# Down projection of an encoder layer as a block product in seven multiplications

## Chip, cores and metric

The kernel runs on one core of one Trainium2 chip. The metric is the device time of one execution in microseconds (us), lower is better. TensorE is called PE, VectorE DVE, ScalarE ACT and GpSimd POOL, as in the profile; SP is the engine that issues most transfers.

## What is computed

One layer of a bidirectional encoder over 768 token rows (512 of a prompt, 256 of a sample), width 1024, all in float32. The change touches the last stage alone, the down projection of the ConvFFN with its residual and the final norm:

```python
uv = dwconv(jnp.matmul(h, w_up), ffn_conv_w, ffn_conv_b, ...)   # (768, 6144)
gate, val = jnp.split(uv, 2, axis=-1)
x = x + jnp.matmul(jax.nn.gelu(gate) * val, w_down)             # (768, 3072) @ (3072, 1024)
y = rmsnorm(x, final_g)
```

## The kernel before

**Numbers in two parts.** Each float32 operand of a large matmul is split into a rounded high part (ACT copies it to the matmul type) and the rest (a subtraction on DVE or POOL). A product is three matmuls: high by high, low by high, high by low. They add up in a PSUM bank.

**Up projection.** `window(j, pend)` (line 1162), 24 times, makes one tile of 128 gate and 128 value channels for all 768 tokens. It is already a block product in seven multiplications: the operands of the next window are sums of weight blocks, made on POOL by `UpSet.sums` (lines 899 to 902) and split by `UpSet.pair` (lines 924, 925). Each window has seven calls of `prod` (line 1096) of twelve 128x384 matmuls. Beside them ACT and DVE finish the tile of the window before (`pend`, class `Gate`): taps of the convolution, gelu, product. `spill` (line 1145) writes the finished tile `vl` to DRAM (`actd`).

**Down projection.** The last loop (line 1317) goes over two halves `h` of 384 tokens. For each half, 24 steps `k` over the 3072 channels: `act` loads the half tile of activations back (line 1274) and splits it (ACT line 1277, DVE line 1278), `unit("down", ...)` loads a 128x1024 slab of `w_down` and splits it (ACT line 106, DVE line 107), and 18 matmuls of 128x512 (three token tiles `c`, two column halves `hf`, three parts, `mms`, line 1330) add into six banks that stay open over the half. Every slab of `w_down` is thus loaded and split twice. After each half `add_res` (line 1300) adds the six banks to the residual rows `x2`, which were loaded back from DRAM.

**Final norm.** `final(c)` (line 1302) for one tile of 128 tokens: two squares with row sums on ACT (line 838), a POOL product with the gain (line 1306), a chain of tiny DVE and ACT instructions for the root (`tok_rstd`, lines 845 to 853), a DVE product (line 1309), an ACT product (line 1310) and two output transfers, issued on ACT's queue. Those of the first half's tiles stand in steps 1 to 3 of the second half; those of the second half come at the end, where the last `TAIL = 4` steps are done tile by tile.

**What sets the order.** In this part each engine runs its instructions in the order of the code. A buffer of a pool is handed on when its last reader is done, so an engine can run ahead of PE by as many steps as there are buffers: eight of tag `v` for the split activations (gate and value tiles, squares and `z` of `final` share them), 14 of tag `u` for split weights, three of `raw` for loaded weights. PSUM has five banks of tag `b` and three of tag `c`.

Of the kernel before, what the change touches and what calls it, by code (L numbers as in the profile page):

```python
# [8 lines left out]
F32 = mybir.dt.float32  # L9
F32R = mybir.dt.float32r  # L10
I32 = mybir.dt.int32
AF = mybir.ActivationFunctionType
# [21 lines left out]
def kernel(  # L34
# [43 lines left out]
    def r32(ap):  # L78
        return ap.bitcast(F32R)
# [10 lines left out]
    def plan(key, src, n):  # L90
        order.append((key, src, n))
# [3 lines left out]
    def issue_to(i):  # L95
        while issued[0] < min(i, len(order)):
            key, src, n = order[issued[0]]
            issued[0] += 1
            raw = rawtile("w_raw")
            nc.sync.dma_start(raw[:, 0:n], src)  # L100
            if key[0] == "gw":
                t = wtile("w_gw")
                hi, lo = t[:, 0:n], t[:, 528 : 528 + n]
            else:
                hi, lo = wtile("w_hi")[:, 0:n], wtile("w_lo")[:, 0:n]
            A.activation(r32(hi), raw[:, 0:n], AF.Copy)  # L106
            (V if key[0] == "down" else G).tensor_tensor(r32(lo), raw[:, 0:n], hi, op=SUB)  # L107
            units[key] = (r32(hi), r32(lo))
# [19 lines left out]
    for i in range(8):  # L128
        plan(("out", i), w_out[i], 1024)

    for h in range(2):
        for k in range(24):
            plan(("down", h, k), w_down[k], 1024)

# [963 lines left out]

    actd = dram.tile([24, P, NP], F32, name="actd")
    ffs = ExitStack()  # L1100
    ffp = None

    def etile(name):
        return ffp.tile([P, HT], F32, tag="e", name=name, bufs=6)

    def vtile(name):
        return ffp.tile([P, NP], F32, tag="v", name=name, bufs=8)

    def gtile(name):
        return ffp.tile([P, 1024], F32, tag="g", name=name, bufs=2)  # L1110

    fw, fb = cs["fw"], cs["fb"]

    class Gate:
# [29 lines left out]
        def spill(self):  # L1144
            nc.sync.dma_start(actd[self.j], self.vl[:])

        def rest(self):

            self.mid(1, 0)
            self.mid(0, 0)  # L1150
            self.taps(0, 0)
            self.gelu(0)
            self.mid(0, 1)
            self.taps(1, 0)
            self.mult(0)
            self.mid(1, 1)
            self.taps(0, 1)
            self.gelu(1)
            self.taps(1, 1)
            self.mult(1)  # L1160

    def window(j, pend):
# [3 lines left out]
        if j + 2 < 24:  # L1166
            sets[j + 2] = UpSet(j + 2)
        p1, q, wv = etile("p1"), etile("q"), etile("wv")
        gt, vl = vtile("gt"), vtile("vl")
# [7 lines left out]
        if nx:  # L1177
            nx.hi_g()
        else:
            act_to(1)  # L1180
        A.activation(p1[:], ba, AF.Copy)
# [7 lines left out]
        if nx:  # L1189
            nx.pair(0)  # L1190
        else:
            issue_down(1)
        pend.mid(1, 1)
# [17 lines left out]
        if nx:  # L1211
            nx.pair(1)
            nx.hi_22()
            nx.lo_22()()
        else:
            act_to(2)
            issue_down(2)
# [47 lines left out]

    acts = {}
    aorder = [(h, k) for h in range(2) for k in range(24)]
    atop = [0]

    def act_to(i):  # L1270
        while atop[0] < min(i, 48):
            h, k = aorder[atop[0]]
            t = ffp.tile([P, HT], F32, tag="ar", name="a_raw", bufs=3)
            nc.sync.dma_start(t[:], actd[k, :, h * HT : h * HT + HT])
            x = vtile("act")
            ah, al = x[:, 0:HT], x[:, HT:NP]
            A.activation(r32(ah), t[:], AF.Copy)
            V.tensor_tensor(r32(al), t[:], ah, op=SUB)
            acts[h, k] = (ah, al)
            atop[0] += 1  # L1280

    def act(h, k):
        act_to(aorder.index((h, k)) + 3)
        return acts.pop((h, k))

    down0 = [o[0] for o in order].index(("down", 0, 0))

    def issue_down(n):
        issue_to(down0 + n)

    for j in range(1, 24):
        pend = window(j, pend)


    fgb = gtile("fgb")

    def add_res(c, ps):
        for hf in range(2):
            xx = x2[c][hf]
            V.tensor_tensor(xx, ps[hf], xx, op=ADD)  # L1300

# [11 lines left out]

    def dbank(tag):
        return pm["p"].tile([P, 512], F32, tag=tag, name="d", bufs=5 if tag == "b" else 3)

    for h in range(2):
        xr = granule("xr")[:].rearrange("p a b -> p (a b)")
        for c in range(3):
            for hf in range(2):  # L1320
                x2[3 * h + c][hf] = xr[:, 1024 * c + 512 * hf : 1024 * c + 512 * hf + 512]
        bk = {}
        tags = "bbbbbc" if h == 0 else "ccbbbb"

        def mms(a, u, c, hf, k):
            if (c, hf) not in bk:
                bk[c, hf] = dbank(tags[2 * c + hf])
            (ah, al), (wh, wl) = a, u
            for i, (x, w) in enumerate(((ah, wh), (al, wh), (ah, wl))):
                PE.matmul(bk[c, hf], lhsT=r32(x[:, c * P : c * P + P]), rhs=w[:, hf * 512 : hf * 512 + 512],  # L1330
                          start=k == 0 and i == 0, stop=k == 23 and i == 2)

        late = []
        for k in range(24 - TAIL):
            a, u = act(h, k), unit("down", h, k)
            for c in range(3):
                for hf in range(2):
                    if h == 0 and k < 2 and (c, hf) == (2, 1):
                        late.append((a, u, c, hf, k))
                    else:  # L1340
                        mms(a, u, c, hf, k)
            if h == 0 and k == 0:
                pend.rest()
            if h == 0 and k == 2:
                pend.spill()
            if h == 0 and k == 4:
                nc.sync.dma_start(fgb[:], fin_g.to_broadcast([P, D]))
            if k == 1:
                for m in late:
                    mms(*m)  # L1350
            if h == 1 and 1 <= k < 4:
                final(k - 1)
            if 6 <= k < 18 and k % 2 == 0:
                c, hf = divmod((k - 6) // 2, 2)
                nc.sync.dma_start(x2[3 * h + c][hf], x2d[3 * h + c, :, hf * 512 : hf * 512 + 512])
        rest = [(act(h, k), unit("down", h, k), k) for k in range(24 - TAIL, 24)]
        for c in range(3):
            for hf in range(2):
                for a, u, k in rest:
                    mms(a, u, c, hf, k)  # L1360
            add_res(3 * h + c, [bk[c, 0], bk[c, 1]])
            if h:
                final(3 * h + c)
    ffs.close()
# [75 lines left out]
```

## Time and profile before

| | |
|---|---|
| median of three runs | 954.53 us (952.23 to 955.11) |
| the profiled execution | 954.8 us, its span 953.1 us |
| PE, DVE, ACT, POOL busy | 95%, 66%, 53%, 42% of the span |
| mean granted TensorE clock | 0.986 |
| up projection, windows 1 to 23 | to 743.5 us from the start of the span |
| down projection | 743.5 to 945.9 us |
| last output | to 953.1 us |

Times in the rows below are microseconds from the start of the span, durations of one instruction are in nanoseconds where the column says so. A row of an idle time names what ended it.

### The profile page before, as it was taken

The page shows a single profiled execution, that of the slowest core. Times are in us where ns is not written, and L with a number is a line of the kernel's source. Part 1 is how long each engine was busy: PE and PEld are TensorE (multiplying, and loading weights), DVE is VectorE, ACT ScalarE, POOL GpSimd, SP SyncE. Part 2 cuts the span into 40 slices and gives each one's busy share as a digit, 9 for nine tenths or more (in the row PEclk, how much of TensorE's full clock was granted, in tenths as well). Part 3 has the DMA queues.
Part 4 walks back from the last instruction along what each step waited for, and adds up shares of the span by engine and source line. Part 5 has one row for each costly group of instructions (what it writes and reads, how often), then busy time and mean ns, then how long its engine had stood idle before and what let it go on. Part 6 is the DMA issues. An engine that isn't in the chain of part 4 may idle for free.

```text
span 953.1 us, 13653 instructions
## 1 busy us (share of the span) xinstructions
PE 908.2 (95%) x5066; PEld 828.5 (87%) x5066; DVE 631.4 (66%) x1176; ACT 500.4 (53%) x827; POOL 403.9 (42%) x261
## 2 busy tenths in 40 slices
PE   8896999999899899899999999999999999999996
PEld 6796877898899677899999999999999788888885
DVE  6788999437778757576766766767667664346523
ACT  6464565055354055575665766756655454336513
POOL 4622333256433516687667667676672000010001
PEclk9998999999899999999999999999999999999999
DMA  6411111063235212323223133132221697428901
GB/s 221 144 46 64 45 67 45 13 157 89 78 87 190 89 47 87 125 70 122 95 88 122 69 114 118 66 122 84 100 78 48 221 355 248 147 91 275 315 29 67
DMA packets 42419, 110.47 MB, mean 116 GB/s; under 512 B 4976, under 2 KB 12656, under 8 KB 42352
## 3 DMA queue, kind: packets, MB, share of 16 engines
q1 hardware_dynamic: 40320, 106.38, 33.6%
q10 hardware_dynamic: 2032, 3.22, 1.0%
q8 instruction: 40, 0.66, 0.3%
q14 instruction: 27, 0.22, 0.1%
HBM read 93.78 MB, written 15.79 MB: 115 GB/s over the span
## 4 chain that ended last, share of the span: by engine, by line
PE 73%; DVE 16%; POOL 3%; ACT 3%; issue 2%; DMA 2%; SPq 0%; POOLq 0%; ACTq 0%; DVEq 0%
PE b L1096 34%; PE d L1330 20%; PE big L141 6%; PE sm L832 3%; PE sm L742 3%; PE b L1035 2%; DVE xc L350 2%; PE sm L451 1%; DVE w L375 1%; POOL hq L955 1%; POOL w_lo L107 1%; DVE thi L386 1%; DVE nt L197 1%; DVE xgl L252 1%; DVE rs L199 1%
## 5 line engine op out<-in xcount | busy, mean ns | idle before, releaser
L1096 PE MATMUL b<-hq,w_sh 128*128 128x384 f32 (+2 forms) x792 | 199.9, 334 | 3.6 <-POOL hq L955 2.7
L1330 PE MATMUL d<-w_hi,act 128*128 128x512 f32 x576 | 179.9, 393 | 2.2 <-DVE vl L1142 1.1
L925 POOL TENSOR_TENSOR w_sl<-w_S,w_sh 128x1024 fp32r<-128x1024 f32 x48 | 115.7, 2410 | 115.7 <-ACT w_sh L924 115.7
L1096 PEld LDWEIGHTS b<-hq,w_sh 128*128 128x128 f32 x792 | 143.1, 189 | 4.3 <-POOL hq L955 3.0
L1096 PE MATMUL b<-hq,w_sl 128*128 128x384 f32 (+2 forms) x396 | 132.3, 334 | 0.0
L1330 PEld LDWEIGHTS d<-w_hi,act 128*128 128x128 f32 x576 | 107.8, 188 | 28.0 <-DVE vl L1142 1.5
L106 ACT ACTIVATE w_hi<-w_raw 128x1024 fp32r<-128x1024 f32 (+1 forms) x77 | 81.0, 1056 | 90.7 <-PE d L1330 52.8
L107 POOL TENSOR_TENSOR w_lo<-w_raw,w_hi 128x1024 fp32r<-128x1024 f32 (+1 forms) x29 | 74.5, 2577 | 118.6 <-ACT w_hi L106 75.0
L1330 PE MATMUL d<-w_lo,act 128*128 128x512 f32 x288 | 112.7, 391 | 0.0
L1096 PE MATMUL b<-hq,w_gh 128*128 128x384 f32 x384 | 99.1, 339 | 0.0
L1306 POOL TENSOR_TENSOR z<-xr,fgb 128x512 f32<-128x512 f32 x6 | 7.8, 1294 | 213.0 <-ACT sq L838 126.5
L107 DVE TENSOR_TENSOR w_lo<-w_raw,w_hi 128x1024 fp32r<-128x1024 f32 x48 | 58.8, 1225 | 56.3 <-ACT w_hi L106 55.2
L1096 PEld LDWEIGHTS b<-hq,w_sl 128*128 128x128 f32 x396 | 74.8, 189 | 0.0
L1096 PEld LDWEIGHTS b<-hq,w_gh 128*128 128x128 f32 x384 | 70.2, 189 | 0.0
L1096 PE MATMUL b<-hq,w_gl 128*128 128x384 f32 x192 | 65.0, 339 | 0.0
L1330 PEld LDWEIGHTS d<-w_lo,act 128*128 128x128 f32 x288 | 54.1, 188 | 12.2
L1124 ACT ACTIVATE cv<-vl,col 128x512 f32<-128x512 f32 (+1 forms) x48 | 32.1, 669 | 49.1 <-DVE vl L1220 47.8
L141 PE MATMUL big<-xgh,w_hi 128*128 128x512 f32 x208 | 54.8, 344 | 2.4 <-DVE kT L762 2.3
L1096 PE MATMUL b<-hq,w_v 128*128 128x384 f32 x288 | 54.4, 337 | 0.9 <-DVE wv L1252 0.9
L141 PE MATMUL big<-xgl,w_hi 128*128 128x512 f32 x208 | 53.5, 338 | 0.0
L141 PE MATMUL big<-xgh,w_lo 128*128 128x512 f32 x208 | 53.3, 337 | 0.0
L1096 PEld LDWEIGHTS b<-hq,w_v 128*128 128x128 f32 x288 | 50.7, 188 | 1.0 <-ACT w_gh L906 1.0
(301 smaller groups left out, 2054.3 us busy)
## 6 DMA issues: line engine op xcount, KB each, us to landing
w_raw<-in_w_down_dram SPq DMA_DIRECT2D x48, 512.0 KB, 4.9
w_g<-in_w_up_dram SPq DMA_DIRECT2D x24, 512.0 KB, 4.1
w_v<-in_w_up_dram SPq DMA_DIRECT2D x24, 512.0 KB, 4.9
actd<-vl SPq DMA_DIRECT2D x24, 384.0 KB, 2.6
a_raw<-actd SPq DMA_DIRECT2D x48, 192.0 KB, 5.1
w_raw<-in_w_fm_dram SPq DMA_DIRECT2D x13, 512.0 KB, 3.4
w_raw<-in_w_out_dram SPq DMA_DIRECT2D x8, 512.0 KB, 5.3
M<-md SPq DMA_DIRECT2D x12, 256.0 KB, 4.1
```

What stands on the lines that cost most here:

```text
L106: A.activation(r32(hi), raw[:, 0:n], AF.Copy)
L107: (V if key[0] == "down" else G).tensor_tensor(r32(lo), raw[:, 0:n], hi, op=SUB)
L141: PE.matmul(dst, lhsT=w, rhs=x[:, lo:hi], start=first and i == 0, stop=last and i == 2,)
L197: V.tensor_tensor(t[:], y, y, op=MUL)
L350: V.scalar_tensor_tensor(xc[:, d0:d1], xs[:, d0 + o : d1 + o], cw[:, 4 * j + i : 4 * j + i + 1], xc[:, d0:d1], op0=MUL, op1=ADD)
L742: PE.matmul(ps[:, 0:256], lhsT=x[:, p0 : p0 + P], rhs=w[:, o : o + 256], start=n == 0, stop=n == 23)
L832: PE.matmul(ps[:, 0:512], lhsT=a, rhs=w[:, hf * 512 : hf * 512 + 512], start=first and k == 0 and i == 0, stop=last and k == n - 1 and i == 2)
L925: G.tensor_tensor(r32(sl[:, 0:1024]), x, sh[:, 0:1024], op=SUB)
L1035: PE.matmul(ps[:, 0:512], lhsT=a, rhs=w[:, hf * 512 : hf * 512 + 512], start=k == 0 and i == 0, stop=k == 3 and i == 2)
L1096: PE.matmul(t[:, a:b], lhsT=wt, rhs=r32(hq[:, k, off + a : off + b]), start=first and n == 0, stop=n == len(seq) - 1, skip_group_check=True)
L1124: A.activation(t[:, 0 : hi - lo], x[:, lo:hi], AF.Identity, bias=fb[:, m : m + 1], scale=fw[:, 48 + m : 49 + m])
L1330: PE.matmul(bk[c, hf], lhsT=r32(x[:, c * P : c * P + P]), rhs=w[:, hf * 512 : hf * 512 + 512], start=k == 0 and i == 0, stop=k == 23 and i ...
```

## The change

The product of activations A (768 x 3072) and weights B (3072 x 1024) is cut in two by two blocks: A by token half (first index, 384 tokens) and by even or odd channel tile (second index), B by even or odd channel tile and by column half. Seven products of size 384 x 1536 x 512 take the place of eight:

- S1 = A21 + A22, S3 = A11 - A21, S2 = S1 - A11, S4 = A12 - S2, and from the weights B12 - B11, B22 - B12, B22 - (B12 - B11) and (B22 - (B12 - B11)) - B21.
- In the order of `DORD`: 1 is A11 B11, 2 is A12 B21, 5 is S1 (B12 - B11), 7 is S3 (B22 - B12), 6 is S2 (B22 - B12 + B11), 3 is S4 B22, 4 is A22 times the last weight sum.

Each product has twelve steps (pairs of channel tiles); a step is 9 matmuls of 128x512 (three token tiles, three parts) into three banks. After a product, `into` adds each bank on DVE to all residual blocks that it belongs to: 4, 1, 2, 2, 3, 1 and 1 blocks for each of three banks, 42 additions in all.

The activation sums are made by `Gate.sums` on POOL, four subtractions or additions of 128x384 for each pair of windows, and written to DRAM; a step of the down projection then loads one 128x384 operand. The weight blocks are loaded once (48 of 128x512) and stay; sums of weights are made in place on POOL. The low part of a weight operand is a POOL subtraction in products 1, 2 and 4; in the others ACT copies the operand to a PSUM bank (`wc`) and DVE subtracts from there. All six residual tiles are loaded at the start of window 23 (`down_begin`). The work left of the last tile and the additions of banks 1 and 2 of a product stand, one entry a step, in the list `todo`; so do `final(0)` to `final(2)`, after product 3. Tag `v` has seven buffers in place of eight.

```diff
-            (V if key[0] == "down" else G).tensor_tensor(r32(lo), raw[:, 0:n], hi, op=SUB)
+            G.tensor_tensor(r32(lo), raw[:, 0:n], hi, op=SUB)
...
+        def sums(self):
+
+            if self.j % 2 == 0:
+                return
+            p = self.j // 2
+            u, v = evens.pop(p), self.vl
+            a11, a21, a12, a22 = u[:, 0:HT], u[:, HT:NP], v[:, 0:HT], v[:, HT:NP]
+            t = ffp.tile([P, 4 * HT], F32, tag="sp", name="sp", bufs=1)
+            s1, s3, s2, s4 = (t[:, HT * i : HT * i + HT] for i in range(4))
+            G.tensor_tensor(s1, a21, a22, op=ADD)
+            G.tensor_tensor(s3, a11, a21, op=SUB)
+            G.tensor_tensor(s2, s1, a11, op=SUB)
+            G.tensor_tensor(s4, a12, s2, op=SUB)
+            spq.append(lambda: nc.sync.dma_start(actd[p, :, 3 * HT : 7 * HT], t[:]))
...
         A.activation(gt[:, 0:HT], ba, AF.Copy)
+        pend.sums()
         prod(bd, w, 4, False)
         V.tensor_tensor(vl[:, 0:HT], bd, q[:], op=ADD)
+        if not nx:
+            prep_to(2)
...
+    DORD = (1, 2, 5, 7, 6, 3, 4)
+    steps = [(i, p) for i in DORD for p in range(12)]
+    ahead = 3
...
+    def down_begin():
+
+        st = wpool.tile([P, 2048], F32, tag="S", name="x_S", bufs=1)
+        homes = [gtile("x_g")[:], gtile("x_g")[:], st[:, 0:1024], st[:, 1024:2048],
+                 rawtile("x_raw")[:, 0:1024], rawtile("x_raw")[:, 0:1024]]
+        load_to(2)
+        for c in range(NT):
+            x2[c] = [homes[c][:, 512 * hf : 512 * hf + 512] for hf in range(2)]
+            nc.sync.dma_start(homes[c], x2d[c])
...
+    def load_to(n):
+
+        while done_load[0] < min(n, len(steps)):
+            i, p = steps[done_load[0]]
+            if i in NEW:
+                wblock(NEW[i], p)
+            t = etile("a_raw")
+            nc.sync.dma_start(t[:], actd[p, :, HT * AOFF[i] : HT * AOFF[i] + HT])
+            xd[i, p] = t
+            done_load[0] += 1
...
+    def prep_to(n):
+
+        while done_prep[0] < min(n, len(steps)):
+            i, p = steps[done_prep[0]]
+            load_to(done_prep[0] + 1)
...
+            elif i == 5:
+                G.tensor_tensor(b11, b12, b11, op=SUB)
+                w = b11
...
             x = vtile("act")
             ah, al = x[:, 0:HT], x[:, HT:NP]
+            wt = wtile("w_s")
+            wh, wl = wt[:, 0:512], wt[:, 528:1040]
+            A.activation(r32(wh), w, AF.Copy)
+            if i in (1, 2, 4):
+                G.tensor_tensor(r32(wl), w, wh, op=SUB)
+            else:
+                ct = cbank("wc")
+                A.activation(ct[:], w, AF.Copy)
+                V.tensor_tensor(r32(wl), ct[:], wh, op=SUB)
             A.activation(r32(ah), t[:], AF.Copy)
             V.tensor_tensor(r32(al), t[:], ah, op=SUB)
...
+    def into(i, c, b):
+        for th, hf in INTO[i]:
+            xx = x2[3 * th + c][hf]
+            if i == 4:
+                V.scalar_tensor_tensor(xx, b, -1.0, xx, op0=MUL, op1=ADD)
+            else:
+                V.tensor_tensor(xx, b, xx, op=ADD)
...
+    for n, i in enumerate(DORD):
+        bk = [bank(), bank(), None]
+        for p in range(12):
+            s = 12 * n + p
+            last = i == 4 and p >= 12 - TAIL
+            if not (last and p > 12 - TAIL):
+                prep_to(s + 1 + ahead)
+            if i == 4 and p == 12 - TAIL:
+                prep_to(len(steps))
+            if not last:
+                for c in range(2):
+                    dmms(bk[c], i, p, c)
+                if p:
+                    if p == 1:
+                        bk[2] = bank()
+                        dmms(bk[2], i, 0, 2)
+                    dmms(bk[2], i, p, 2)
+            if todo:
+                todo.pop(0)()
...
+        if i == 4:
             for c in range(3):
+                for p in range(12 - TAIL, 12):
+                    dmms(bk[c], i, p, c)
+                into(i, c, bk[c])
+                final(3 + c)
+        else:
+            into(i, 0, bk[0])
+            todo += [(lambda i=i, c=c, b=bk[c]: into(i, c, b)) for c in (1, 2)]
+            if i == 3:
+                todo += [(lambda c=c: final(c)) for c in range(3)]
```

How the change moves instructions shows at two places. The first is ACT, where the final norm of the first half's tiles stands among the preparations of later steps (`w_hi` or `w_s` is a weight split, `act` an activation split, `sq`, `rt` and `z` belong to `final`). Before, in the second half's steps 1 to 3:

```order
L106 ACTIVATE w_hi<-w_raw 128x1024
L838 ACTIVATE sq,s_8286<-xr 128x512 x2
L848 ACT_TABLE_LOAD
L848 ACTIVATE rt<-s_8286,pre 128x1
L1310 ACTIVATE z<-z,rt 128x512
L1311 DMA out_dram<-z 128x512
L1312 DMA out_dram<-xr 128x512
L1277 ACTIVATE act<-a_raw 128x384
L106 ACTIVATE w_hi<-w_raw 128x1024
L838 ACTIVATE sq,s_8335<-xr 128x512 x2
```

Now, in the third, fourth and fifth step of the last product:

```order
L1354 ACTIVATE act<-a_raw 128x384
L834 ACTIVATE sq,s_9134<-x_g 128x512 x2
L844 ACT_TABLE_LOAD
L844 ACTIVATE rt<-s_9134,pre 128x1
L1373 ACTIVATE z<-z,rt 128x512
L1374 DMA out_dram<-z 128x512
L1375 DMA out_dram<-x_g 128x512
L1347 ACTIVATE w_s<-w_d 128x512
L1354 ACTIVATE act<-a_raw 128x384
L834 ACTIVATE sq,s_9171<-x_g 128x512 x2
```

One preparation still stands between two finals, but it is now that of a step of 9 matmuls, where it was that of a step of 18. The second place is POOL from the last window into the down projection (`w_S` and `w_sl` are weights of the up projection, `sp` the activation sums). Before:

```order
L899 TENSOR_TENSOR w_S<-w_g,w_v 128x512
L900 TENSOR_TENSOR w_S<-w_v 128x512
L901 TENSOR_TENSOR w_S<-w_S,w_g 128x512
L902 TENSOR_TENSOR w_S<-w_g,w_S 128x512
L925 TENSOR_TENSOR w_sl<-w_S,w_sh 128x1024 x2
L1306 TENSOR_TENSOR z<-xr,fgb 128x512 x6
```

Now:

```order
L921 TENSOR_TENSOR w_sl<-w_S,w_sh 128x1024 x2
L1159 TENSOR_TENSOR sp<-vl 128x384
L1160 TENSOR_TENSOR sp<-vl 128x384
L1161 TENSOR_TENSOR sp<-sp,vl 128x384
L1162 TENSOR_TENSOR sp<-vl,sp 128x384
L1349 TENSOR_TENSOR w_s<-w_d,w_s 128x512 x8
...
L1349 TENSOR_TENSOR w_s<-w_d,w_s 128x512 x16
L1329 TENSOR_TENSOR w_d<-w_d 128x512 x12
L1332 TENSOR_TENSOR w_d<-w_d 128x512 x12
L1335 TENSOR_TENSOR w_d<-w_d 128x512 x12
L1338 TENSOR_TENSOR w_d<-w_d 128x512 x12
L1349 TENSOR_TENSOR w_s<-w_d,w_s 128x512 x6
```

POOL had only the six products of the final norm in this stage; it now has an instruction of 128x512 for every step, and the four sums of a pair follow the weights of every second window.

## Rows read from the trace of the kernel before

**Rows 1.** The page: busy time and share of each engine.
```profile
PE 908.2 (95%) x5066; PEld 828.5 (87%) x5066; DVE 631.4 (66%) x1176; ACT 500.4 (53%) x827; POOL 403.9 (42%) x261
```

**Rows 2.** The page: the chain that ended last, by engine.
```profile
PE 73%; DVE 16%; POOL 3%; ACT 3%; issue 2%; DMA 2%; SPq 0%; POOLq 0%; ACTq 0%; DVEq 0%
```

**Rows 3.** That chain in order of time: start, length, what, how many.
```profile
752.53 0.70 DVE vl L1142
...
753.27 192.65 PE d L1330 x834
945.94 0.70 DVE xr L1300
```

**Rows 4.** Stretches of the down projection: length, busy time by engine, clock, DMA share, GB/s.
```profile
743.50:753.30 9.80, 7.64 (x33) 5.33 (x31) 7.54 (x11) 5.83 (x9) 0.00 (x0) 1.00 0.59 214
753.30:945.90 192.60, 192.60 (x834) 156.46 (x834) 94.62 (x141) 81.29 (x124) 7.76 (x6) 1.00 0.58 196
763.00:783.00 20.00, 20.00 (x89) 16.28 (x88) 14.05 (x18) 12.20 (x16) 0.00 (x0) 1.00 0.98 351
```

**Rows 5.** The page's transfer issues: KB each, median us from issue to landing.
```profile
a_raw<-actd SPq DMA_DIRECT2D x48, 192.0 KB, 5.1
```

**Rows 6.** Groups of instructions in two windows, 700 to 724: busy us, mean ns, idle before.
```profile
L919 DVE TENSOR_TENSOR w_gl<-wc,w_gh 128x512 fp32r<-128x512 f32 x4 | 2.7, 679 | 0.0
L902 POOL TENSOR_TENSOR w_S<-w_g,w_S 128x512 f32<-128x512 f32 x2 | 2.6, 1297 | 0.2
L931 ACT ACTIVATE w_v<-w_v 128x512 fp32r<-128x512 f32 x2 | 1.2, 614 | 0.0
L935 ACT ACTIVATE wc<-w_v 128x512 f32<-128x512 f32 x2 | 1.2, 602 | 0.0
```

**Rows 7.** POOL in order of time in the windows: start, length, idle before.
```profile
704.72 2.40 POOL L925 TENSOR_TENSOR w_sl<-w_S,w_sh 128x1024 fp32r<-128x1024 f32 x1 [3.39 <-ACT w_sh L924]
...
719.46 2.40 POOL L925 TENSOR_TENSOR w_sl<-w_S,w_sh 128x1024 fp32r<-128x1024 f32 x1 [3.84 <-ACT w_sh L924]
722.59 2.41 POOL L925 TENSOR_TENSOR w_sl<-w_S,w_sh 128x1024 fp32r<-128x1024 f32 x1 [0.73 <-ACT w_sh L924]
```

**Rows 8.** Groups of instructions, 743.5 to 953.1: the same columns.
```profile
L1278 DVE TENSOR_TENSOR act<-a_raw,act 128x384 fp32r<-128x384 f32 x46 | 25.4, 553 | 6.3 <-ACT act L1277 6.3
L1277 ACT ACTIVATE act<-a_raw 128x384 fp32r<-128x384 f32 x46 | 23.7, 514 | 7.8 <-DMA a_raw<-actd 4.0 <-PE d L1330 1.3 <-issue 1.0
L1300 DVE TENSOR_TENSOR xr<-d,xr 128x512 f32<-128x512 f32 x12 | 8.3, 690 | 33.6 <-PE d L1330 33.6
L838 ACT ACTIVATE sq<-xr 128x512 f32<-128x512 f32 x12 | 7.5, 624 | 21.5 <-DVE xr L1300 19.4 <-DVE pre L845 2.1
```

**Rows 9.** POOL and DVE in order of time, an early stage and a window.
```profile
59.57 0.96 DVE L376 SCALAR_TENSOR_TENSOR thi<-thi,xc 128x768 f32<-128x768 f32 x1
63.10 2.55 POOL L107 TENSOR_TENSOR w_lo<-w_raw,w_hi 128x1056 fp32r<-128x1056 f32 x1 [16.64 <-PE sm L451]
63.35 3.12 DVE L375 SCALAR_TENSOR_TENSOR w<-w,thr 128x768 f32<-128x768 f32 x1
719.93 0.49 DVE L1133 SCALAR_TENSOR_TENSOR cv<-gt,col,cv 128x255 f32<-128x255 f32 x1
```

**Rows 10.** ACT in order of time, finals in the second half's first steps.
```profile
850.41 1.28 ACT L848 ACT_TABLE_LOAD   x1 [4.08 <-DVE pre L845]
...
856.22 0.61 ACT L838 ACTIVATE sq<-xr 128x512 f32<-128x512 f32 x1
...
860.06 0.53 ACTq L1312 DMA_DIRECT2D out_dram<-xr  x1
...
862.03 0.62 ACT L838 ACTIVATE sq<-xr 128x512 f32<-128x512 f32 x1
```

**Rows 11.** The last output transfer, issued on SP.
```profile
949.28 0.34 SPq L1312 DMA_DIRECT2D out_dram<-xr  x1
```

**Rows 12.** A PE wait before the windows and the clock behind it.
```profile
383.66 0.39 PE L1096 MATMUL b<-hq,w_sh 128*128 128x256 f32 x1 [2.66 <-POOL hq L955]
384.00:386.00 2.00, 2.00 (x12) 2.00 (x11) 1.84 (x7) 1.17 (x4) 2.00 (x2) 0.50 0.46 184
```

More of the change, by code (lines that the diff above doesn't have):

```diff
@@ L1097, in prod @@
                       start=first and n == 0, stop=n == len(seq) - 1, skip_group_check=True)
-    actd = dram.tile([24, P, NP], F32, name="actd")
+    actd = dram.tile([12, P, 7 * HT], F32, name="actd")
     ffs = ExitStack()
@@ L1106, in vtile @@
     def vtile(name):
-        return ffp.tile([P, NP], F32, tag="v", name=name, bufs=8)
+        return ffp.tile([P, NP], F32, tag="v", name=name, bufs=7)
     def gtile(name):
@@ L1264 @@
     pend = Gate(0, gt, vl)
[L1266 to L1274, printed above, removed]
+    DORD = (1, 2, 5, 7, 6, 3, 4)
+    AOFF = {1: 0, 2: 1, 4: 2, 5: 3, 7: 4, 6: 5, 3: 6}
+    steps = [(i, p) for i in DORD for p in range(12)]
+    ahead = 3
@@ new lines, in wblock @@
+    def wblock(b, p):
+        if (b, p) not in wB:
+            if b == 11:
+                if p % 2 == 0:
+                    wu[p // 2] = wtile("w_d")
+                t = wu[p // 2][:, 528 * (p % 2) : 528 * (p % 2) + 512]
+            else:
+                if p % 6 == 0:
+                    wu[b, p // 6] = granule("w_d")[:].rearrange("p a b -> p (a b)")
+                t = wu[b, p // 6][:, 512 * (p % 6) : 512 * (p % 6) + 512]
+            r, c = divmod(b, 10)
+            nc.sync.dma_start(t, w_down[2 * p + r - 1, :, 512 * c - 512 : 512 * c])
+            wB[b, p] = t
+        return wB[b, p]
@@ L1278, in act_to @@
             V.tensor_tensor(r32(al), t[:], ah, op=SUB)
[L1279 to L1289, printed above, removed]
+            ops[i, p] = (r32(ah), r32(al), r32(wh), r32(wl))
+            done_prep[0] += 1
+            load_to(done_prep[0] + 2)
     for j in range(1, 24):
         pend = window(j, pend)
-    fgb = gtile("fgb")
@@ L1297, in add_res @@
[L1297 to L1300, printed above, removed]
+    fgb = rawtile("fgb")
     def final(c):
@@ L1312, in final @@
         (nc.sync if c == NT - 1 else nc.scalar).dma_start(out[c, :, 512:1024], xx)
[L1314 to L1335, printed above, removed]
-            for c in range(3):
[L1337 to L1363, printed above, removed]
@@ new lines, with dmms @@
+    INTO = {1: ((0, 0), (0, 1), (1, 0), (1, 1)), 2: ((0, 0),), 5: ((0, 1), (1, 1)), 7: ((1, 0), (1, 1)),
+            6: ((0, 1), (1, 0), (1, 1)), 3: ((0, 1),), 4: ((1, 0),)}
+    def into(i, c, b):
[3 more added lines that the diff above has]
+                V.scalar_tensor_tensor(xx, b, -1.0, xx, op0=MUL, op1=ADD)
+            else:
+                V.tensor_tensor(xx, b, xx, op=ADD)
+    def dmms(b, i, p, c):
+        ah, al, wh, wl = ops[i, p]
+        for n, (x, w) in enumerate(((ah, wh), (al, wh), (ah, wl))):
+            PE.matmul(b[:], lhsT=x[:, c * P : c * P + P], rhs=w,
+                      start=p == 0 and n == 0, stop=p == 11 and n == 2)
```

62 lines of the change are left out of this document (38 added, 24 removed).

## The prediction

> **What bounds the kernel now.** I read the page first: PE is busy for 95% of the span [rows 1], and PE instructions make 73% of the chain that ended last [rows 2]. The chain in order of time says the same of the stage that changes: from 753.27 us it is one run of 834 down-projection matmuls without a gap, 192.65 us long [rows 3], so one 128x512 matmul starts each 192.65 / 834 = 0.231 us. [...] The first 30 of the 864 matmuls were no such run. They took 9.77 us, from 743.5 us to 753.27 us, where 30 x 0.231 = 6.93 us would do: the chain stood in the last tile's convolution and product (DVE L1142), which held a bank that the half wanted [rows 3, 4]. So PE's count of matmuls sets this stage as long as the operands are ready.
>
> **The change part by part.** The sum is made against the profiled execution, 954.8 us, which lies 0.3 us above the median of the three runs.
>
> *Fewer matmuls.* Seven products of 12 steps of 9 matmuls are 756 where there were 864, all 128x512: 108 x 0.231 = **24.9 us less**. Nothing hides behind PE here, so this counts in full.
>
> *The start.* The first product needs three banks instead of six, the third in its second step, so the wait for the last tile's work goes: 9.77 - 6.93 = **2.8 us less**. What is late next is POOL's queue. It holds eight low parts and then the last pair's four sums, which wait for DVE's last product of the tile, some four steps or 9 us in; four sums of 1.0 us and a low part later, at 14 to 15 us, step 8 is ready, which PE wants at 8 x 2.08 = 16.6 us. On SP's queue the spill of these sums holds the loads of step 11: issued at 14 us, landed 5.1 us later [rows 5], split in 2 us, against 11 x 2.08 = 22.9 us. Both have 1 to 2 us to spare. Bounds 0 and 2 us, taken **0.5 us more**.
>
> *The windows.* Sums of 128x384 have no row. POOL needs 1.30 us for 512 columns [rows 6] and 2.41 us for 1024 [rows 7], so about 1.0 us for 384, 4.1 us in every second window. A window is 719.46 - 704.72 = 14.74 us, and POOL sits idle 3.84 + 0.73 us in it, waiting for ACT [rows 7]. The sums push the next window's weight sums by 4.1 us, which takes that wait and some of ACT's slack; the split weights are used a window later. Taken at 0; without that cover, up to 1 us in each of 11 windows.
>
> *Preparing a step.* PE needs 9 x 0.231 = 2.08 us for a step. ACT spends 0.60 us on the high part, 0.60 us on the copy to PSUM (products 5, 7, 6, 3) and 0.51 us on the activation, 1.7 us [rows 6, 8]. DVE spends 0.55 us on the activation and, in those products, 0.68 us on the weight [rows 6, 8]. POOL has 1.30 us in every step. A step loads at most 459 kB, 221 GB/s at this pace, against 351 GB/s seen [rows 4]. Each is under 2.08 us, but two of them are not independent: a DVE instruction that reads two SBUF operands does not run beside POOL. One that takes 0.96 us alone took 3.12 us from 63.35 us: it waited for the POOL instruction that ended at 65.65 us. One that reads an operand from PSUM took its 0.49 us beside a POOL instruction of 2.40 us [rows 7, 9]. So the activation's split and POOL's instruction take turns, 0.55 + 1.30 = 1.85 us a step together: still under 2.08 us, but a lost lead comes back at only 0.2 us a step. [...]
>
> *The additions.* 42 x 0.69 us [rows 8] = 29 us of DVE in place of 8. They stand in DVE's queue: the first of a product waits for its bank, and later splits queue behind it. When it waits, DVE has prepared the three steps beyond the product, so that PE has some 7.6 us of work; after product 1 (four additions a bank) the third split comes 8.3 + 3 x 0.55 us plus waits for POOL later, when PE wants it after 11.8 us. Products 1 and 6 (three a bank, beside 1.23 us of splits a step) come near the margin, the others do not. Bounds 0 and 6 us, taken **1.5 us more**.
>
> *Finals of the first half's tiles.* Each holds ACT from its squares to its last transfer's issue, 860.06 + 0.53 - 856.22 = 4.4 us, and the first loads a table for 1.28 us more [rows 10]. Before, a step was 18 matmuls, 4.2 us, and finals 5.8 us apart (862.03 - 856.22) were caught up by the splits made ahead [rows 10]. Now a step is 2.08 us. Let t count from the first matmul of the last product. The first squares run at once, the root waits until DVE has added bank 2 and split step 77, about t = 2.5. From there table 1.3, the rest of the final 4.4 - 1.2 = 3.2 (squares 0.62 each [rows 8]), and twice a preparation (1.05) and a final (4.4): ACT is free for step 80 at t = 17.9, and its weight is copied at 18.5. Four steps remain; with POOL and DVE in turn the last is ready at 18.5 + 4 x 1.85 = 25.9, with POOL alone counting at 18.5 + 4 x 1.30 = 23.7. PE, tile by tile, wants it at 8 x 2.08 + 3 x 0.69 = 18.7, so it waits 5.0 to 7.2 us. Bounds 2 (the lead covers most of it) and 8 us (the clock falls in the wait), taken **6.0 us more**.
>
> *The end.* The last tiles come 12 x 0.231 = 2.8 us apart in place of 5.5, but a final takes ACT 4.4 us, so they queue: the third starts 8.8 us after the first, PE ends 5.5 us after it, and each has both squares behind its addition (0.6 us more) instead of one. Before, 953.1 - 945.9 = 7.2 us passed from the last matmul to the end, 3.8 of them after the issue of the last transfer [rows 3, 11]. Now it is 8.8 + 0.6 + 7.2 - 5.5 = 11.1 us, **3.9 us more**, bounds 3 and 5.
>
> The sum: -24.9 - 2.8 + 0.5 + 1.5 + 6.0 + 3.9 = -15.8 us, **939.0 us**.
>
> **The rivals.**
> - *The finals of the first half stay hidden*, as the three before did: no PE wait in the last product, 939.0 - 6.0 = 933.0 us. For it: the run of rows 3 has no wait. Against it: a step is half as long. Chance 0.17.
> - *More lost at the borders of products*: if POOL takes the lead from DVE, a quarter to a half of the 29 us of additions lies open, 939.0 - 1.5 + 7 to 14.5 = 944.5 to 952 us. Chance 0.13.
> - *DVE becomes the bound, and the kernel is slower.* In products 5, 7, 6 and 3 DVE has 0.68 + 0.55 us a step and the wait for POOL. It decides from a mean wait of 2.08 - 1.23 = 0.85 us on; at a whole POOL instruction, 1.30 us, a step takes 2.53 us, 48 x 0.45 = 21.6 us more, and the 24 additions of these products lie open too, 16.6 us: 939.0 - 1.5 + 38.2 = 975.7 us. For it: the full wait at 63.35 us [rows 9]. Against it: POOL works 1.30 of 2.08 us, so a wait at a random time is 0.4 us in the mean, and 0.6 us where POOL's instructions follow each other. Chance 0.08.
> - *The windows stretch*, 1 us in 11 of them: 950 us, chance 0.04. *The loads bound the first products*, being smaller pieces: some 5 us, 944 us, chance 0.03.
> - [...] That the change does less than it says is out: the order of the program holds 756 matmuls.
>
> **How the numbers follow.** The forecast with its own terms, 934 to 943 us, has 0.55. The range of 930 to 949 us takes in the hidden finals, the loads and the lower half of the open additions; it leaves out the slow case, the windows at their worst and the rest of the additions. A measurement of this kernel can tell about 0.3% (3 us) from no change. Faster by more: 0.55 + 0.17 + 0.03 + 0.12 of the open additions = 0.87; same: the windows and the rest of the additions, 0.05; slower 0.08.
>
> **What would show it.** 756 matmuls of the down projection at 0.231 us; no PE wait in the first steps; POOL busy some 120 us in the stage; DVE's activation splits longer than 0.55 us in the mean; PE waits of 1 to 2 us each in the last steps, 5 to 7 us in all, for POOL's or DVE's splits; 11 us from the last matmul to the end. A pace of steps well above 2.08 us in the middle products, or PE waits in the windows, would make it wrong.

## The result, and the profile of the changed kernel

The changed kernel takes 959.95 us in the median (958.48 to 964.71, 8 runs), the kernel before 954.53 us (952.23 to 958.46, 8 runs). The ratio is 1.0058, with a 95% interval of 1.0036 to 1.0080: **0.6% slower**, where 939.0 us and a faster kernel were forecast. The profiled execution took 960.48 us with a span of 958.8 us. Two executions of some 3000 us, one of e7's kernel and one of the kernel before in the runs beside e9 to e12, are left out of every figure below.

First the page of the changed kernel, the lines that answer to [rows 1] and [rows 2].

```profile
PE 890.9 (93%) x4958; PEld 811.8 (85%) x4958; DVE 682.4 (71%) x1242; ACT 539.2 (56%) x947; POOL 571.1 (60%) x393
...
PE 65%; DVE 17%; POOL 6%; issue 4%; ACT 4%; DMA 3%; SPq 0%; ACTq 0%; DVEq 0%; POOLq 0%
```

There are 108 matmuls less, as announced, and PE is busy for 17 us less; yet the span grew by 5.7 us. PE's share of the chain fell from 73% to 65%. So PE waits. Where, the matmuls in order of time tell: start, length, number, and in brackets the idle time ahead and what ended it. The first row is the one that answers to [rows 12], ahead of the windows; the others are the down projection.

```profile
384.75 0.50 PE L1092 MATMUL b<-hq,w_sh 128*128 128x256 f32 x1 [2.67 <-POOL hq L951]
...
744.62 17.45 PE L1392 MATMUL b<-w_s,act 128*128 128x512 f32 x74
763.55 9.94 PE L1392 MATMUL b<-w_s,act 128*128 128x512 f32 x41 [1.48 <-POOL w_s L1349]
773.65 1.43 PE L1392 MATMUL b<-w_s,act 128*128 128x512 f32 x5 [0.16 <-DVE act L1355]
777.62 76.76 PE L1392 MATMUL b<-w_s,act 128*128 128x512 f32 x324 [2.54 <-DVE x_S L1387]
868.80 66.05 PE L1392 MATMUL b<-w_s,act 128*128 128x512 f32 x276 [14.42 <-DVE x_S L1387]
936.13 0.49 PE L1392 MATMUL b<-w_s,act 128*128 128x512 f32 x1 [1.27 <-ACT act L1354]
937.57 4.33 PE L1392 MATMUL b<-w_s,act 128*128 128x512 f32 x9 [0.94 <-DVE act L1355]
942.24 6.28 PE L1392 MATMUL b<-w_s,act 128*128 128x512 f32 x26 [0.35 <-DVE act L1355]
```

All 756 matmuls are there. At 0.231 us they would take 174.6 us; from 744.62 to 942.24 + 6.28 = 948.52 us they took 203.9. The difference of 29.3 us is 21.2 us of waits (the brackets) and 8.1 us of slower matmuls. One wait, 14.42 us in front of the 445th matmul, is half of it all.

Most of the slower matmuls stand behind waits. The stretches behind the two longest give length, busy time of PE, granted clock, DMA share and GB/s:

```profile
777.60:780.60 3.00, 2.98 (x7) 0.50 0.93 306
780.60:783.60 3.00, 3.00 (x14) 0.97 0.95 327
783.60:800.00 16.40, 16.40 (x72) 1.00 0.83 256
...
868.80:871.80 3.00, 3.00 (x7) 0.50 0.39 119
871.80:874.80 3.00, 3.00 (x12) 0.81 0.24 71
```

After the wait of 2.54 us and after that of 14.42 us the granted clock is at 0.50 for three to four microseconds (the 0.81 is a mean: about one more microsecond at 0.50) and then comes back. The 324 matmuls from 777.62 us took 76.76 us where 324 x 0.231 = 74.8 would do, the 276 from 868.80 us 66.05 where 63.8 would do: 1.9 and 2.3 us.

**The large wait.** Four engines around it, in order of time. POOL first:

```profile
831.67 1.61 POOL L1332 TENSOR_TENSOR w_d<-w_d 128x512 f32<-128x512 f32 x1 [6.21 <-DMA w_d<-in_w_down_dram]
...
835.07 17.33 POOL L1335 TENSOR_TENSOR w_d<-w_d 128x512 f32<-128x512 f32 x12
852.35 14.78 POOL L1338 TENSOR_TENSOR w_d<-w_d 128x512 f32<-128x512 f32 x12
```

POOL's queue holds nothing but weight sums here. When the last block of product 7 has landed, it runs the twelve sums of product 6 and the twelve of product 3 in one go, until 867.13 us, far ahead of the steps that want them. ACT:

```profile
854.93 0.63 ACT L1347 ACTIVATE w_s<-w_d 128x512 fp32r<-128x512 f32 x1 [13.14 <-POOL w_d L1338]
```

This is the high part of step 50, the third of product 6. What it reads, POOL's third sum of product 6, was there at some 839.4 us (835.07 + 3 x 17.33 / 12). Yet it waited 13.14 us, until the second sum of *product 3* ended (the first began at 852.35 us, one takes 1.23). The two have no operand in common. But the split weights (`w_s`) and the first block's tiles (`w_d` of `wtile`) come from the same fourteen buffers. The first block's first tile holds the blocks of the first two steps, and its last reader is the second sum of product 3 (line 1338), which reads what product 6 left there. So it seems that step 50's tile was given that buffer: the wait ends with that reader, and e1 puts it to the test. DVE:

```profile
843.91 1.05 DVE L1355 TENSOR_TENSOR act<-a_raw,act 128x384 fp32r<-128x384 f32 x1
856.15 0.69 DVE L1353 TENSOR_TENSOR w_s<-wc,w_s 128x512 fp32r<-128x512 f32 x1 [11.19 <-POOL w_d L1338]
856.76 10.79 DVE L1355 TENSOR_TENSOR act<-a_raw,act 128x384 fp32r<-128x384 f32 x1
867.48 1.27 DVE L1387 TENSOR_TENSOR x_S<-b,x_S 128x512 f32<-128x512 f32 x2
```

Step 50's activation split stands on DVE from 856.76 to 867.55 us: 10.79 us for what takes 0.54 us alone. It ends 0.4 us after POOL's run of sums, of which eight began while it stood there (one every 14.78 / 12 = 1.23 us). Behind it in DVE's queue are the additions of product 7, which empty the banks that PE wants; that is why the bracket of PE names x_S, line 1387. So the wait has, as it seems from these rows, two links in series: a buffer, and a DVE instruction that POOL kept out.

**The start** lost 33.0 - 120 x 0.231 = 5.3 us up to 777.62 us. DVE's last product of the last tile, the sums on POOL that wait for it, and then ACT's and SP's queues:

```profile
756.24 0.42 DVE L1140 TENSOR_TENSOR vl<-cv,gt 128x256 f32<-128x256 f32 x1
```
```profile
757.08 1.33 POOL L1159 TENSOR_TENSOR sp<-vl 128x384 f32<-128x384 f32 x1
...
761.07 1.21 POOL L1162 TENSOR_TENSOR sp<-vl,sp 128x384 f32<-128x384 f32 x1
```
```profile
767.26 0.63 ACT L1347 ACTIVATE w_s<-w_d 128x512 fp32r<-128x512 f32 x1 [8.30 <-DMA w_d<-in_w_down_dram]
```
```profile
756.69 0.32 SPq L1148 DMA_DIRECT2D actd<-vl  x1
762.30 0.32 SPq L1163 DMA_DIRECT2D actd<-sp  x1
762.68 0.42 SPq L1301 DMA_DIRECT2D w_d<-in_w_down_dram  x1
```

DVE's product ends at 756.66 us, 12.0 us into the stage (from 744.62), and the four sums of the last pair at 762.28, 17.7 us into it. Step 8's low part is behind them (PE waits 1.48 us), and SP holds the next weight block behind their spill: ACT waits 8.30 us for it.

**The last product**: its last 36 matmuls took 948.52 - 934.85 = 13.7 us (8.3 at full pace). Of the 5.4 us more, 2.6 are waits (1.27, 0.94 and 0.35) and 2.8 slower matmuls; the nine from 937.57 us ran at a mean clock of 0.62:

```profile
937.50:942.00 4.50, 4.22 (x9) 0.62 0.02 5
```

The end is 958.8 - 948.52 = 10.3 us after the last matmul, in place of 7.2.

### The profile page after: what moved, and what is told of

Same layout as the page of the kernel before. It is cut to its first block, busy times and chain, and to the rows that moved or that the text cites. A ratio compares the mean times of both kernels' runs of the same rounds, so it can differ in the third digit from the quotient of the medians.

```text
span 958.8 us, 13896 instructions
## 1 busy us (share of the span) xinstructions
PE 890.9 (93%) x4958; PEld 811.8 (85%) x4958; DVE 682.4 (71%) x1242; ACT 539.2 (56%) x947; POOL 571.1 (60%) x393
## 4 chain that ended last, share of the span: by engine, by line
PE 65%; DVE 17%; POOL 6%; issue 4%; ACT 4%; DMA 3%; SPq 0%; ACTq 0%; DVEq 0%; POOLq 0%
PE b L1092 35%; PE b L1392 10%; PE big L137 6%; PE sm L828 3%; PE sm L738 3%; PE b L1031 2%; PE sm L447 2%; POOL w_d L1335 2%; DVE xc L346 1%; DVE act L1355 1%; DMA a_raw<-actd 1%; POOL hq L951 1%; POOL w_lo L107 1%; DVE nt L193 1%; DVE thi L382 1%
## 5 line engine op out<-in xcount | busy, mean ns | idle before, releaser
L1392 PE MATMUL b<-w_s,act 128*128 128x512 f32 x756 | 182.6, 402 | 21.3 <-DVE x_S L1387 17.0
L1392 PEld LDWEIGHTS b<-w_s,act 128*128 128x128 f32 x756 | 144.2, 192 | 59.4 <-DVE x_S L1387 17.8
L1355 DVE TENSOR_TENSOR act<-a_raw,act 128x384 fp32r<-128x384 f32 x84 | 89.7, 1085 | 16.2 <-ACT act L1354 14.1
L1349 POOL TENSOR_TENSOR w_s<-w_d,w_s 128x512 fp32r<-128x512 f32 x36 | 51.1, 1443 | 68.5 <-ACT w_s L1347 66.8
L1347 ACT ACTIVATE w_s<-w_d 128x512 fp32r<-128x512 f32 x84 | 52.1, 620 | 27.7 <-POOL w_d L1338 13.1
L1354 ACT ACTIVATE act<-a_raw 128x384 fp32r<-128x384 f32 x84 | 43.4, 517 | 21.5 <-PE b L1392 11.0
L920 ACT ACTIVATE w_sh<-w_S 128x1024 fp32r<-128x1024 f32 x48 | 50.3, 1047 | 2.2 <-POOL w_S L896 1.5
```

The costliest lines, as they stand in the source:

```text
L920: A.activation(r32(sh[:, 0:1024]), x, AF.Copy)
L1347: A.activation(r32(wh), w, AF.Copy)
L1349: G.tensor_tensor(r32(wl), w, wh, op=SUB)
L1392: PE.matmul(b[:], lhsT=x[:, c * P : c * P + P], rhs=w, start=p == 0 and n == 0, stop=p == 11 and n == 2)
```

## The experiments

Theory A: the two links above make the wait of 14.42 us, and each can be taken away by itself. Theory B: DVE has too much to do with its 42 additions, and the wait is what it owes. Later a rival C to A's second link: the 10.8 us have another cause than DVE's two SBUF operands.

### e1: the first block's buffers kept to the end

```diff
+    junk = tiny.tile([P, 8], F32, tag="jk", name="jk", bufs=1)
+    for n in range(6):
+        G.tensor_copy(junk[:, n : n + 1], wu[n][:, 0:1])
     ffs.close()
```

> Edit: the six tiles that hold the first weight block are read once more at the very end (six one-column copies on GpSimd), so no step's split weight can be given one of their buffers. Theory A (two links in series make the 14.4 us PE wait at 854 us: step 50's high part waits until 854.9 us for a buffer whose last reader is product 3's second weight sum, and then the activation's split is shut out by GpSimd's unbroken run of sums until 867.1 us): the first link goes, the second stays. ACT has no wait of 13 us for a weight sum; one activation split still lasts as long as a run of sums, up to 15 us, against a lead of three steps (6.2 us): PE wait 4 to 9 us in place of 14.4, time 950 to 956 us. Theory B (DVE simply has too much to do, the 42 additions above all): the wait moves but keeps its size, 958 to 962 us.

Measured: 944.29 us (943.29 to 944.94, 4 runs), ratio to the kernel before 0.988 (0.9851 to 0.9909). Better than either theory had it. Two of this kernel's PE rows, in order of time:

```profile
...
763.91 11.19 PE L1392 MATMUL b<-w_s,act 128*128 128x512 f32 x46 [1.38 <-POOL w_s L1349]
777.64 141.63 PE L1392 MATMUL b<-w_s,act 128*128 128x512 f32 x600 [2.55 <-DVE x_S L1387]
...
```

The large wait is gone entirely: 600 matmuls in one run, and ACT no longer waits for a sum of product 3. That shows the first link. POOL's run of sums is still there, but now DVE and POOL took turns all through it; the line of the activation splits (shortest, median and longest in ns) shows none above 1.7 us:

```profile
L1355 DVE TENSOR_TENSOR act<-a_raw,act x84: 539/1052/1662, 743.5 to 925.0; 128x384 fp32r<-128x384 f32 x84
```

POOL's twelve sums of product 3 took 18.37 us in place of 14.78, so they gave way too:

```profile
853.05 18.37 POOL L1338 TENSOR_TENSOR w_d<-w_d 128x512 f32<-128x512 f32 x12
```

B is out: DVE has the same instructions here. The second link, as A had put it, does not come by itself from a run of sums.

### e2 and e6: a small POOL instruction between the sums of product 3

```diff
...
                 G.tensor_tensor(b21, b11, b21, op=SUB)
+                G.memset(gp[:], 0.0)
```

> Edit: a one-column memset on GpSimd behind each of product 3's twelve weight sums, the buffers as in the change. Theory A: the first link stays (step 50's high part at about 855 us or 1 us later), but DVE gets its turn between two sums, so the split of 10.8 us falls below 2 us: PE wait 3 to 6 us in place of 14.4, time 949 to 952 us. Theory B: no effect, 958 to 962 us. If GpSimd keeps DVE out across the small instruction as well, the split stays near 10 us and the time at 960.

Measured: 958.31 us in the median (948.49 to 963.04, 10 runs), no difference from the kernel before, but in two groups: 948.5, 949.4, 949.6 and 952.9 us, and six from 957.9 to 963.0. The profiled execution was the 948.5. The same kernel once more, for a profile of the other group:

> The kernel with the memset behind each sum of product 3 once more, for its profile: its ten executions fell into two groups, 948.5 to 952.9 and 957.9 to 963.0 us, and the profiled one was of the first, with no split above 1.7 us. Theory A: a profile of the second group shows one activation split of about 10 us during the run of product 3's sums and a PE wait of 13 to 15 us in place of 4.5; one of the first group shows neither. Rival C: the 10 us lie elsewhere.

This one took 961.87 us. The activation splits and the wait of PE, first of the 948.5 us execution (e2):

```profile
L1357 DVE TENSOR_TENSOR act<-a_raw,act x84: 540/1050/1666, 740.8 to 928.4; 128x384 fp32r<-128x384 f32 x84
```
```profile
856.68 66.19 PE L1394 MATMUL b<-w_s,act 128*128 128x512 f32 x276 [4.51 <-DVE x_S L1389]
```

and of the 961.9 us execution (e6):

```profile
L1357 DVE TENSOR_TENSOR act<-a_raw,act x84: 537/1048/11180, 745.6 to 941.9; 128x384 fp32r<-128x384 f32 x84
```
```profile
870.32 66.04 PE L1394 MATMUL b<-w_s,act 128*128 128x512 f32 x276 [14.84 <-DVE x_S L1389]
```

The same program, once with and once without a split of 11.18 us, and the wait of PE differs by 14.84 - 4.51 = 10.3 us. That prices both links in these two executions: the buffer about 4.5 us, the exclusion (DVE kept out by POOL) about 10.3. The memset did not end the exclusion, as A had expected it to in every execution. In e6 the split, begun at 857.89 us, was passed over by eight sums that began after it, with a memset ahead of each; the running one and the last:

```profile
857.27 1.30 POOL L1339 TENSOR_TENSOR w_d<-w_d 128x512 f32<-128x512 f32 x1
858.50 0.11 POOL L1340 MEMSET gp<- 128x1 f32 x1
...
867.40 1.25 POOL L1339 TENSOR_TENSOR w_d<-w_d 128x512 f32<-128x512 f32 x1
868.60 0.09 POOL L1340 MEMSET gp<- 128x1 f32 x1
```

### e3 and e4: both, and sums that can't run ahead

e3 is e1 and e2 together. In e4 the buffers are kept, and a one-column copy ahead of each sum of products 6 and 3 makes POOL wait for a step already prepared:

```diff
...
+            if i in (6, 3):
+                G.tensor_copy(gp[:], ops[steps[done_prep[0] - 8]][3].bitcast(F32)[:, 0:1])
```

> Both edits, the kept buffers and the memset behind each sum of product 3. Theory A: no wait of more than 2 us is left between products 7 and 3, time 944 to 947 us. Theory B: 955 or more.

> Kept buffers, and ahead of each sum of products 6 and 3 a one-column copy on GpSimd of the low part that DVE made for the step eight steps before, so that the sums can't run further ahead than eight steps and come one by one. Theory A: as with both edits before, no activation split above 2 us in products 6 and 3, time 944 to 947 us. Theory B: 955 or more.

Measured: e3 946.11 us (944.22 to 948.85, 4 runs), e4 943.49 us (941.49 to 945.19, 4 runs). Neither is told apart from e1's 944.29: with the buffers kept, they won nothing that these runs show. No split in e4 exceeds 2 us, as expected (longest 1.67 us), but none does in e1 either.

### e5: product 6's activation split reads PSUM

The buffers are those of the change; only the DVE instruction that was kept out has one SBUF operand now, for which ACT makes one more copy in each step of product 6.

```diff
+            if i in (6,):
+                cx = cbank("xc")
+                A.activation(cx[:, 0:HT], t[:], AF.Copy)
+                V.tensor_tensor(r32(al), cx[:, 0:HT], ah, op=SUB)
+            else:
                 V.tensor_tensor(r32(al), t[:], ah, op=SUB)
```

> Edit: in product 6 alone the activation's low part is taken from a copy in PSUM that ACT makes (one more ACT instruction of about 0.5 us a step); the buffers are as in the change, so step 50 still waits for product 3's second sum (about 855 us). Theory A (the second link is GpSimd keeping a DVE instruction with two SBUF operands out, now and then for a whole run of sums): such a wait can't occur in product 6, the PE wait falls from 14.4 to 3 to 5 us in every execution, time 947 to 951 us with a spread of a few us. Rival C (the 10.8 us have another cause than the two SBUF operands: the additions, a missing buffer, a late activation): the split or its neighbour still takes about 10 us, time 956 to 963 us.

Measured: 948.64 us (946.24 to 950.49, 4 runs), ratio 0.9932 (0.9912 to 0.9952). The splits from PSUM, POOL's run of sums beside them, and the PE wait:

```profile
L1358 DVE TENSOR_TENSOR act<-xc,act x12: 541/550/558, 839.8 to 870.5; 128x384 fp32r<-128x384 f32 x12
```
```profile
849.13 15.02 POOL L1338 TENSOR_TENSOR w_d<-w_d 128x512 f32<-128x512 f32 x12
```
```profile
855.50 66.59 PE L1397 MATMUL b<-w_s,act 128*128 128x512 f32 x276 [3.88 <-DVE x_S L1392]
```

The buffer's 3.9 us stay, the ten microseconds are gone: all four executions are below 951 us, where all eight of the changed kernel are above 958. No split from PSUM took more than 0.56 us, though six of them began during this run of sums. C, with its 956 to 963 us, is out, and A's second link stands, with one reserve: the copy on ACT moves times as well, and e2 shows that the exclusion can stay away (four of ten executions) with two SBUF operands. Times moved by as much, with both operands in SBUF, were not tried.

### e7 and e12: the last pair's sums and spills later

With the buffers kept, the four sums come one a step in steps 6 to 9 and both spills in step 10.

```diff
...
-            lambda: g.sums(), lambda: (g.spill(), spq.pop()())]
+            lambda: None]
+    late = []
+    todo += [lambda: late.extend(g.sums(True)), lambda: late[0](), lambda: late[1](), lambda: late[2](),
+             lambda: late[3](), lambda: (g.spill(), spq.pop()())]
```

> Kept buffers (as e1), and the last pair's four sums one a step in steps 6 to 9 and its two spills in step 10, in place of all in steps 4 and 5. If the start loses 5.2 us because the sums hold GpSimd's queue and the spill on SP's queue the loads behind it: no wait for a low part at step 8 (1.4 us), no wait of 8 us of ACT for a weight block, and the additions after product 1 are no longer late (2.5 us): time 3 to 5 us below the 944.3 of e1, 939 to 941 us. If the additions on DVE, taking turns with GpSimd, make the 2.5 us by themselves: only 1.4 us less, 943 us.

> e7's kernel once more, for its profile (the one taken before was of a disturbed execution): at the start no PE wait above 0.5 us, and ACT's wait for a weight block behind the spill below 2 us, time 937 to 941 us.

Measured: 937.7, 938.1 and 940.1 us in e7 (ratio 0.9829, 0.9812 to 0.9846), and 938.43 us in e12, some 6 us below e1. The start in e12's profile:

```profile
743.12 28.28 PE L1394 MATMUL b<-w_s,act 128*128 128x512 f32 x120
772.15 140.07 PE L1394 MATMUL b<-w_s,act 128*128 128x512 f32 x600 [0.75 <-DVE x_S L1389]
```

One wait of 0.75 us is left (a little above the 0.5 that was expected), and the first 120 matmuls take 28.28 us, near 27.7 at full pace. So the start's loss came from where the sums and the spill stood in the queues, and most of the 2.5 us behind product 1's additions came from there too. ACT's wait behind the spill did not fall below 2 us, as had been expected; it moved to a later step and fell from 8.30 to 5.12 us, and a new wait of ACT, 5.98 us for one of the late sums, came beside it. PE lost no more than the 0.75 us by them:

```profile
773.63 0.63 ACT L1349 ACTIVATE w_s<-w_d 128x512 fp32r<-128x512 f32 x1 [5.12 <-DMA w_d<-in_w_down_dram]
```

### e8 and e9: the finals of the first half

The buffers are kept in both. e8 cuts each final into three pieces (squares; root; product and transfers) and hands them out over steps 74 to 80. e9 besides takes their scratch and products out of the seven buffers of the split activations, issues their second transfer on SP, and does three of the last tiles' squares in product 3.

```diff
...
-                todo += [(lambda c=c: final(c)) for c in range(3)]
+                todo += [lambda: fin1(0), lambda: fin2(0), lambda: (fin3(0), fin1(1)), lambda: fin2(1),
+                         lambda: (fin3(1), fin1(2)), lambda: fin2(2), lambda: fin3(2)]
```

> Kept buffers (as e1), and the finals of the first half's tiles in three pieces each (squares; root; product and transfers), one or two pieces a step from step 74 to 80, so that ACT doesn't wait for DVE between them. If the finals' hold of ACT makes the 4.8 us of waits in the last product (1.3 + 0.9 + 0.4 and the gaps between): ACT prepares steps 80 to 83 some 4 us earlier, no PE wait above 0.5 us there, time 939 to 942 us. If the work and not the waiting fills ACT: less than 1.5 us, 943 us.

> Kept buffers (as e1), the finals in pieces (as e8), and besides: their scratch and products in the tile that the sums' spill left free, so that they hold none of the seven buffers of the split activations; their second transfer on SP's queue, so that ACT doesn't wait for DVE's last product; the squares of the other half of tiles 3 to 5 in product 3. In e8 ACT still waited for both, and gained nothing. If these two are what holds ACT: the PE waits of the last product fall from 4.6 to under 2 us, and the end after the last matmul from 10 to about 8 us: time 938 to 941 us. If ACT's own work fills it: 943.

Measured: e8 944.23 us (943.31 to 945.04, 4 runs), no gain on e1 where 939 to 942 was expected; e9 938.59 us (937.39 to 941.12, 4 runs), ratio 0.9824 (0.9798 to 0.9850). Two rows of ACT in e8 show what held it: a buffer that PE had to give back, and a transfer issued on ACT that waited for DVE's last product, so that the next square came late.

```profile
905.55 0.53 ACT L1354 ACTIVATE act<-a_raw 128x384 fp32r<-128x384 f32 x1 [1.50 <-PE b L1402]
...
911.40 0.63 ACT L834 ACTIVATE sq<-x_g 128x512 f32<-128x512 f32 x1 [1.31 <-DVE x_g L1376]
```

In e9 one wait of the last product is left, and the end is 937.3 - 929.77 = 7.5 us behind the last matmul:

```profile
921.90 7.87 PE L1410 MATMUL b<-w_s,act 128*128 128x512 f32 x26 [1.51 <-DVE act L1355]
```

### e10 and e11: all together

> Kept buffers, the start of e7 and the finals of e9 together. The two lie 150 us apart and should add up: e7's 939.1 less what e9 gains against e1's 944.3 (0 to 6 us): 933 to 939 us.

> As e10, with e4's one-column copies that let GpSimd's sums of products 6 and 3 run no more than eight steps ahead. If DVE's waits for GpSimd in products 6 and 3 cost nothing once the buffers are kept: the same as e10 within 2 us; if they still cost: 2 to 4 us less.

Measured: e10 932.46 us (931.22 to 940.68, 6 runs), ratio 0.978 (0.9744 to 0.9815); e11, with e4's pacing, 931.78 us (930.93 to 933.93, 4 runs), ratio 0.9753 (0.9732 to 0.9774), not told apart from e10 in the median. The gains add up: 944.29 - 6.2 (e7) - 5.7 (e9) = 932.4. But e10 has two groups again: four executions from 931.2 to 932.6 us, and two of 939.7 and 940.7 at a mean clock of 0.974 in place of 0.983 to 0.985. Neither of the two has a profile, so whether DVE was kept out in them, with the buffers kept, is open; e11's four executions have no such case, which is too few to say that its pacing prevents it. The down projection of e10's profile, of the first group, in order of time:

```profile
741.47 28.32 PE L1412 MATMUL b<-w_s,act 128*128 128x512 f32 x120
770.47 143.30 PE L1412 MATMUL b<-w_s,act 128*128 128x512 f32 x610 [0.68 <-DVE x_S L1407]
915.28 6.33 PE L1412 MATMUL b<-w_s,act 128*128 128x512 f32 x26 [1.51 <-DVE act L1357]
```

So a kernel with the seven products is some 2% faster than the one before, once the queues and buffers around them are right: e10's median is 22 us below the kernel before and 27 below the change as it was made. The kernel before was not given e9's edits to its finals, so not all of the 22 us is shown to be the products'; its end after the last matmul was 7.2 us already.

## Why the prediction was wrong

By its own steps, with the times of the profiled execution:

- *Fewer matmuls, 24.9 us less*: right. 756 at a pace of 0.231 us wherever nothing waited.
- *The start*: mis-sized. The three waits for the last tile's work went, as forecast, but 5.3 us came in their place where 0.5 was taken and 2 was the upper bound. The step named the right queues (eight low parts, then four sums; the spill ahead of the loads). It had the sums done and step 8's low part behind them at 14 to 15 us; the sums alone ended at 17.7. DVE's last product of the tile, for which they wait, was done at 12.0 us in place of 9, and they took 5.2 us together in place of 4.0, as DVE's splits took their turns among them. The margin of 1 to 2 us that the step gave was eaten by that, and e7 took 6 us out by moving them. Of the 5.3 us, 2.5 are the wait behind product 1's additions, for which the sum has a term of its own.
- *The windows*: right. From the matmul behind the POOL wait ahead of the windows to the down projection's first it is 744.62 - 384.75 = 359.9 us; before, 743.5 - 383.66 = 359.8 [rows 4, 12].
- *Preparing a step*: here it failed, in the rule that it drew from one row. It took from one row [rows 9] that a DVE instruction with two SBUF operands waits for the POOL instruction that is running and then has its turn, so that the two take "1.85 us a step together". Two more such instructions of the kernel before, of 0.94 us alone, took 3.05 us from 70.79 and 3.15 us from 141.88, each ending 0.8 us after the POOL instruction that ran when it began. Mostly so: the median split was 1.05 us, and e1's longest 1.66. But one was passed over for a whole run of sums, 10.79 us. The mean of 1.09 us (89.7 us over 84) is about what the step had expected; the one wait was not. The two groups of e2 and, with the reserve made there, e5 show it.
- *The additions*: the step that failed first. Its sum rests on "DVE has prepared the three steps beyond the product, so that PE has some 7.6 us of work". That lead wasn't there. Step 50's weights waited for a buffer whose last reader belongs to step 61, and DVE stood idle for 11.19 us with the lead running out. The prediction took the three steps as prepared without asking for their buffers: weights kept for later products and weights of the step share one set of fourteen. In place of 1.5 us for all borders, that of products 7 and 6, which the step had not counted among those near the margin, cost 14.4 us, and the slower clock behind this wait and the one after product 1 cost 4.2. e1 mends this one step and takes the exclusion away with it, which gives the price of the buffer with all that hung on it: 959.95 - 944.29 = 15.7 us.
- *Finals of the first half*: right in the queue that holds PE up, and near in size, 13.7 - 8.3 = 5.4 us where 6.0 was taken; that the size came out so near is in part luck. The step expected 5.0 to 7.2 us of waits, and had the clock in its bound of 8 alone; there were 2.6 us of waits and 2.8 of slower matmuls. e8 adds what the step left out: with the wait for DVE's root chain spread out, the activation's buffers and a transfer's wait hold ACT as long.
- *The end*: 10.3 us where 11.1 was taken.

Of the rivals, "DVE becomes the bound" had the right instruction and the right wait, but as a mean over 48 steps, at a whole POOL instruction each. "More lost at the borders of products" had the right place and the wrong cause. Neither asked what the margin of 0.2 us a step is worth when the lead is lost in one event of 14 us. What the prediction took from its rows for the two kinds of operand held in the changed kernel, but for one split. Its 48 weight splits that read PSUM took 0.69 us at the longest and 0.68 in the median, 19 of them begun while a POOL instruction ran. Of its 84 activation splits, from two SBUF operands, 46 took more than 0.6 us; each of these began while a POOL instruction ran, and 45 of them ended 0.4 us after that instruction. The other, of 10.79 us, ended 10.2 us after it: eight sums that began later went ahead of it, as eight did in e6.

With the buffers kept (e1), the kernel is at 944.3 us, within the range of 930 to 949 and 5 us above the forecast, about what the start lost.

## What to carry to other kernels

Count the lead of a pipeline in buffers, not in steps: list for each tile that a step needs who read its buffer last, and whether that reader belongs to a later step than the one that waits; a shared set of buffers can tie a step to work eleven steps on. A queue that runs ahead without a limit, as POOL's sums did, is no free prefetch: here it held a buffer and a DVE instruction back from the step that was due. And put work that is needed late, as the last sums and their spill were, late in an in-order queue, one piece a step, rather than all at once ahead of what is needed next.

## What the runs showed of the hardware that was not expected

A DVE instruction with two SBUF operands that met POOL in an unbroken run of sums was passed over until the run ended, 10.79 us in the changed kernel and 11.18 us in e6, while in e1 and in e2's profile the same pair took turns, with 1.67 us at the longest. A POOL memset of 0.1 us between the sums did not free it, and in that kernel both outcomes occurred in the same program, in executions some 10 us apart. In both profiles that show it, DVE had been idle for 11.19 and 9.98 us while POOL ran; in e2's profile, which doesn't show it, for 11.25 us. What tips it is open. After waits of PE of 2.5 and 14.4 us the clock was at 0.50 for three to four microseconds in both cases, so that each cost about 2 us on top (1.9 and 2.3), the short one nearly as much as the long one.
